# Chunk 0's gate and up products as seven block products over two halves of its tokens, in an encoder step on one NeuronCore

## Chip, core and metric

The kernel runs on one NeuronCore of a Trainium2 chip (trn2). The metric is the device time of one execution in microseconds (us). Engines are named as the profile names them: PE (TensorE, matmuls) and PEld (its weight loads), DVE (VectorE), ACT (ScalarE), POOL (GpSimd), SP (SyncE, whose queue issues nearly all DMAs here).

## What is computed

One layer of an encoder for 1152 tokens (1024 of a prompt, 128 of running streams) of width 1024:

```
x = x + 1/2 * SwiGLU_1(RMSNorm(x))
x = x + mixer(RMSNorm(x))            # gated delta rule heads and trailing-mean pooling heads
x = x + 1/2 * SwiGLU_2(RMSNorm(x))
y = RMSNorm(x)
SwiGLU(h) = (silu(h @ Wg) * (h @ Wu)) @ Wd     # Wg, Wu: 1024 x 2816, Wd: 2816 x 1024
```

The change concerns `h @ Wg` and `h @ Wu` of both SwiGLUs. All values are float32. A float32 operand is split into two parts (a rounded one and the rest, `hi` and `lo`), and a product is three matmuls: hi*hi, hi*lo, lo*hi.

## The kernel before

Tokens lie in the free dimension, in three chunks (`CHUNKS`): chunk 0 with 512 tokens, chunks 1 and 2 with 320 each. The 2816 hidden columns are 22 **rows** `f` of 128. For a row the weights are four blocks: g1, g2 (gate, first and second half of the 1024 inputs) and u1, u2 (up). A block has 4 tiles of 128x128, so that `product` (L292) of one block with one operand is 4 x 3 = 12 matmuls, each with a weight load of its own. `piece` (L275) turns a block, or the sum of two, into hi and lo: a copy on ACT (L288) and a subtraction on DVE (L289), with the sum before it on POOL (L283, L287). Pieces go round a ring of seven buffers.

**Chunks 1 and 2** are computed together by a Strassen-Winograd scheme: the two halves of the inputs by the two chunks form a 2x2 block matrix, and seven products replace eight. Its seven operands (B11, T1, B21, B22, T2, T3, T4) are sums and differences of the normalised activations. `operands` (L320) builds them, `combine` (L299) makes the sums. A row of chunks 1 and 2 thus takes 7 pieces and 7 products of 12 matmuls of 320 columns. **Chunk 0** is computed plainly: 4 products of 12 matmuls of 512 columns a row, from the operand tiles `H0` in the buffers A0 to A3.

`gate_up` (L342) runs one SwiGLU's gate and up in three stages:

- **Plain rows**, L498: rows 0 to 7 (`AHEAD = 8`), chunk 0 alone. Beside them `operands` runs in steps (`next(build)`), two steps a row.
- **Mixed rows**, L514: rows 8 to 21, each with 7 products for chunks 1 and 2 and 4 for chunk 0, one row after the other. A row has 8 pieces, since u1 alone is needed for chunk 0.
- **Rows of the other chunks**, L539: rows 0 to 7 for chunks 1 and 2, in a software pipeline: the next row's first product (`fifth`) stands before the row's sixth, and the row's last (`left_up`) after the next row's third. The `yield` at L535 stands before this stage. There the caller (`half_step`, L746) queues 14 transfers that bring chunk 0's finished rows back from DRAM into A0 to A6, for the down projection. They are issued two at a time, each pair behind a row's weight load (`pace`, L151; `load(f, 2)`).

`gated` (L357) stores the finished rows of chunks 1 and 2. Rows 0 to 7 are stored as they are. Of the others, each pair of rows goes through `combine` first, for the down projection, in steps (`step()`): 4 calls in a mixed row, 3 in a row of the last stage. A step there is a DVE operation, a copy on ACT (L370) into one of two buffers `go`, a subtraction (L371) and a DMA out. `down0` (L559) is the down projection of chunk 0. It starts with three weight loads and reads the 14 rows, and it adds its results to the `x` of chunk 0, which has stayed in the buffers x00 and x01. `down12` follows for chunks 1 and 2.

Two matters set the order of the instructions. Each engine executes its own queue in order; the framework orders the queues from the program text, so that a piece can stand ahead of an operation that comes earlier in the text but is ready later. PSUM has four tags a to d with two buffers each (`pt`).

Of the kernel before, what the change touches and what calls it, by code (L numbers as in the profile page):

```python
# [16 lines left out]
KT = D // P  # L17
# [23 lines left out]
def trunk(ctx: ExitStack, tc: tile.TileContext, xin, s0, convst, poolst, cm_in, vec_in, small_in,  # L41
# [257 lines left out]
    def combine(l1, l2, r1, r2, put):  # L299
# [7 lines left out]
        V.tensor_sub(r1, r2, r1)  # L307
# [6 lines left out]
        put("T3", r1)  # L314
        yield
        V.scalar_tensor_tensor(l2, r2, -1.0, l2, ALU.mult, ALU.subtract)
        put("T4", l2)
        yield
# [22 lines left out]

    def gate_up(wi, wg, wu, gk, H, RB, cs, ahead, norm, x0=None):  # L342
# [14 lines left out]
        def gated(f, c, t):  # L357

            q, i = f // 2, 2 * (c - 1) + f % 2
            if f < ahead:  # L360
                SY.dma_start(gk[1][q][:, i * N:(i + 1) * N], t)
                return
            rows.setdefault(q, {})[i] = t
            if len(rows[q]) < 4:
                return

            def put(name, src):
                j = DOWN.index(name)
                go = gs.get("go", 2, N)
                A.copy(go[:, 0], src)  # L370
                (V if name[0] == "B" else G).tensor_sub(go[:, 1], src, go[:, 0].bitcast(F32))  # L371
                SY.dma_start(gk[2][q - ahead // 2][j].rearrange("p (s n) -> p s n", s=2), go.bitcast(F32))

            sums.append(combine(*[rows[q][i] for i in range(4)], put))
# [10 lines left out]
        def gated0(f, pg, pu):  # L385

            sg, su, go = cs.get("sg", N0), cs.get("su", N0), cs.get("go", 2, N0)
# [5 lines left out]
            A.copy(go[:, 0], sg)  # L393
            G.tensor_sub(go[:, 1], sg, go[:, 0].bitcast(F32))  # L394
            SY.dma_start(gk[0][f].rearrange("p (s n) -> p s n", s=2), go.bitcast(F32))
            yield
# [7 lines left out]
        def fifth(w):  # L404

            be, sm, c3 = pt("c")[:, :N], gs.get("sum", 512), gs.get("c3", N)
            product(be, piece(w[2], w[3], more=(sm, w[0])), op["T1"])
            A.mul(c3, be, -1.0)
            return c3, sm

        def left_gate(al, g1, g2):

            p1, ga = gs.get("p1", N), pt("b")[:, :N]
            w1 = piece(g1)
            product(al, w1, op["B11"])
            A.copy(p1, al)
            w2 = piece(g2)
            product(ga, w2, op["B21"])
            V.tensor_add(p1, p1, ga)
            A.activation(p1, p1, AF.Silu)  # L420
            return p1, w1, w2

        def right_gate(al, sm, g2, c3):

            c2, de = gs.get("c2", N), pt("d")[:, :N]
            product(al, piece(sm), op["T2"], False)
            V.tensor_sub(c2, al, c3)
            product(de, piece(sm, g2), op["B22"])
            V.tensor_add(c2, c2, de)
            A.activation(c2, c2, AF.Silu)  # L430
            return c2

        def right_up(f, al, g1, u1, c2, c3):

            product(al, piece(g1, u1), op["T3"], False)
            V.tensor_sub(c3, c3, al)
            V.tensor_mul(c2, c2, c3)
            gated(f, 2, c2)

        def left_up(f, al, w4, p1):  # L440

            product(al, w4, op["T4"], False)
            V.scalar_tensor_tensor(p1, al, -1.0, p1, ALU.mult, ALU.mult)
            gated(f, 1, p1)
# [5 lines left out]
        op = {}  # L450
        build = operands(wi, op)
        def opening():
# [45 lines left out]
        for f in range(2 if x0 else 0, ahead):  # L498
            g1, g2, u1, u2 = load(f)
            pg, pu = pt("b")[:, :N0], pt("a")[:, :N0]  # L500
            done = gated0(f, pg, pu)
            product(pg, piece(g1), H0[0], True, False)
            product(pg, piece(g2), H0[1], False, True)
            next(done)
            product(pu, piece(u1), H0[0], True, False)
            next(build, None)
            product(pu, piece(u2), H0[1], False, True)
            next(done)
            next(build, None)
# [4 lines left out]
        for f in range(ahead, NF):  # L514
            g1, g2, u1, u2 = w = load(f)
            c3, sm = fifth(w)
            al = pt("a")[:, :N]
            p1, w1, w2 = left_gate(al, g1, g2)
            pg, pu = pt("b")[:, :N0], pt("c")[:, :N0]
            done = gated0(f, pg, pu)  # L520
            product(pg, w1, H0[0], True, False)
            product(pg, w2, H0[1], False, True)
            next(done)
            step()
            c2 = right_gate(al, sm, g2, c3)
            step()
            product(pu, piece(u1), H0[0], True, False)
            step()
            right_up(f, al, g1, u1, c2, c3)
            w4 = piece(u2)  # L530
            product(pu, w4, H0[1], False, True)
            next(done)
            step()
            left_up(f, al, w4, p1)
        yield  # L535

        last = None
        nxt = None
        for f in range(ahead):  # L539
            if not nxt:  # L540
                w = load(f, 2)
                nxt = w, fifth(w)
            (g1, g2, u1, u2), (c3, sm) = nxt
            al = pt("a")[:, :N]
            p1, _, _ = left_gate(al, g1, g2)
            if last:
                left_up(last[0], last[1], piece(last[2]), last[3])
            step()
            c2 = right_gate(al, sm, g2, c3)
            step()  # L550
            if f + 1 < ahead:
                w = load(f + 1, 2)
                nxt = w, fifth(w)
            right_up(f, al, g1, u1, c2, c3)
            last = f, al, u2, p1
            step()
        left_up(last[0], last[1], piece(last[2]), last[3])

    def down0(wd, parts, beside, done):  # L559
# [22 lines left out]
        for _ in W["raws"]:  # L582
            more(0)
# [29 lines left out]
    def down12(wd, gk, op0, beside, done):  # L613
# [15 lines left out]
        def ask(g, tags):  # L629
# [3 lines left out]
            for j, (name, tag) in enumerate(zip(DOWN, tags)):  # L633
                t = region(tag, F32R)
                op[name] = [[t[:, (2 * k + s) * N:(2 * k + s + 1) * N] for k in range(n)] for s in range(2)]
                for k in range(n):
                    pending.append(lambda t=t, j=j, k=k: SY.dma_start(
                        t[:, 2 * k * N:2 * (k + 1) * N].bitcast(F32), gk[2][q - AHEAD // 2 + k][j]))
# [75 lines left out]
    AHEAD = 8  # L714

    def half_step(wi, wg, wu, gk):
# [10 lines left out]
        cs.place(region("A4"), ("sg", N0, 2), ("su", N0, 1), ("rb", N0, 1))  # L727
# [18 lines left out]
        fetch(0, gk[0], ORDER[:14], *[f"A{i}" for i in range(7)])  # L746
        for _ in run:
            pass
        rest()

    def downs(wd, gk, src, done0=None, after0=lambda: (), done12=None, ends=lambda: None):
        op0, stage = {}, []

        def first():

            for q in range(AHEAD // 2):
# [7 lines left out]
        def sums():  # L764
            for q in range(AHEAD // 2):
# [967 lines left out]
```

## Time and profile before

| what | us |
|---|---|
| median of 3 runs (2147.2 to 2149.79) | 2149.47 |
| the profiled execution's own time | 2148.53 |
| its span in the profile | 2146.7 |
| PE busy, of the span | 2116.3 (99%) |
| DVE busy | 1528.7 (71%) |
| ACT busy | 925.8 (43%) |
| POOL busy | 498.4 (23%) |

The granted TensorE clock is at full speed in nearly all of the span. A busy PE means that matmuls are in flight; since they are pipelined, their rate is read from the start times of one block of matmuls and the next, not from the busy time or the mean duration. In the timeline, consecutive matmuls with the same output tag are merged into one row with their count, and the row's duration reaches to the end of the last, so that starts are compared with starts. The first SwiGLU's gate and up takes the stretch from about 5 to 523 us: plain rows to 99 us, mixed rows to 425 us, the other chunks' rows to 523 us. The second's takes the stretch from about 1364 to 1866 us in the same order. Down projections and the mixer fill the rest.

### The profile page before, as it was taken

The page shows a single profiled execution, that of the slowest core. Times are in us where ns is not written, and L with a number is a line of the kernel's source. Part 1 is how long each engine was busy: PE and PEld are TensorE (multiplying, and loading weights), DVE is VectorE, ACT ScalarE, POOL GpSimd, SP SyncE. Part 2 cuts the span into 40 slices and gives each one's busy share as a digit, 9 for nine tenths or more (in the row PEclk, how much of TensorE's full clock was granted, in tenths as well). Part 3 has the DMA queues.
Part 4 walks back from the last instruction along what each step waited for, and adds up shares of the span by engine and source line. Part 5 has one row for each costly group of instructions (what it writes and reads, how often), then busy time and mean ns, then how long its engine had stood idle before and what let it go on. Part 6 is the DMA issues. An engine that isn't in the chain of part 4 may idle for free.

```text
span 2146.7 us, 33093 instructions
## 1 busy us (share of the span) xinstructions
PE 2116.3 (99%) x12355; PEld 1914.3 (89%) x12355; DVE 1528.7 (71%) x2828; ACT 925.8 (43%) x1886; POOL 498.4 (23%) x471
## 2 busy tenths in 40 slices
PE   8999999999999999999999998999999999999998
PEld 7899999999889987887999998889999999988997
DVE  7966666687437887878687876786666668644877
ACT  7433333344213455645555445443333335422333
POOL 1433333351001200100111100243333344100121
PEclk9999999999999999999999999999999999999998
DMA  7333333474465732122222222433333337436572
GB/s 257 118 122 112 118 118 112 143 243 142 126 232 180 270 90 71 51 70 61 79 73 83 64 87 93 167 117 107 118 116 120 113 137 246 145 114 243 188 272 79
DMA packets 102672, 289.70 MB, mean 135 GB/s; under 512 B 16240, under 2 KB 24304, under 8 KB 102256
## 3 DMA queue, kind: packets, MB, share of 16 engines
q1 hardware_dynamic: 101216, 286.24, 39.7%
q8 instruction: 97, 1.59, 0.3%
q10 hardware_dynamic: 1296, 1.36, 0.2%
q14 instruction: 63, 0.52, 0.1%
HBM read 214.89 MB, written 72.66 MB: 134 GB/s over the span
## 4 chain that ended last, share of the span: by engine, by line
PE 89%; DVE 5%; DMA 3%; ACT 1%; POOL 1%; issue 1%; SPq 0%; POOLq 0%; DVEq 0%; ACTq 0%
PE ps_a L59 33%; PE ps_b L59 21%; PE ps_d L59 18%; PE ps_c L59 16%; DVE O L187 1%; DMA B<-g_keep 1%; PE ps_b L63 1%; DMA x<-g_keep 1%; DVE O L289 0%; DVE B L1000 0%; DVE B L769 0%; ACT O L186 0%; DVE A L1139 0%; DVE A L1140 0%; DVE x L656 0%
## 5 line engine op out<-in xcount | busy, mean ns | idle before, releaser
L59 PE MATMUL ps_a<-B,O 128*128 128x320 f32 x3040 | 504.5, 309 | 0.3
L59 PEld LDWEIGHTS ps_a<-B,O 128*128 128x128 f32 x3040 | 463.3, 188 | 9.1 <-issue 0.8
L59 PE MATMUL ps_a<-A,O 128*128 128x320 f32 (+1 forms) x1952 | 424.4, 352 | 1.7 <-DVE x L656 1.4
L59 PEld LDWEIGHTS ps_a<-A,O 128*128 128x128 f32 x1952 | 328.1, 188 | 35.3 <-ACT O L288 1.8
L289 DVE TENSOR_TENSOR O<-Q,O 128x512 fp32r<-128x512 f32 (+1 forms) x238 | 199.4, 840 | 175.6 <-ACT O L288 174.6
L59 PE MATMUL ps_b<-A,O 128*128 128x512 f32 (+1 forms) x1128 | 263.9, 387 | 5.8 <-ACT O L288 5.8
L59 PEld LDWEIGHTS ps_b<-A,O 128*128 128x128 f32 x1128 | 208.0, 188 | 46.2 <-ACT O L288 6.0
L59 PE MATMUL ps_d<-A,O 128*128 128x512 f32 x1056 | 244.2, 391 | 1.6 <-DVE x L607 0.4
L59 PEld LDWEIGHTS ps_d<-A,O 128*128 128x128 f32 x1056 | 196.8, 188 | 47.8 <-ACT O L186 3.0
L288 ACT CAST O<-Q 128x512 fp32r<-128x512 f32 (+1 forms) x238 | 143.1, 605 | 201.2 <-PE ps_c L59 54.7
L289 DVE TENSOR_TENSOR O<-R,O 128x512 fp32r<-128x512 f32 (+1 forms) x216 | 196.3, 912 | 35.7 <-ACT O L288 34.8
L59 PE MATMUL ps_d<-B,O 128*128 128x320 f32 (+1 forms) x1104 | 201.8, 329 | 1.8 <-ACT B L1027 1.0
L288 ACT CAST O<-R 128x512 fp32r<-128x512 f32 (+1 forms) x216 | 131.4, 611 | 144.9 <-PE ps_a L59 56.7
L59 PE MATMUL ps_c<-A,O 128*128 128x512 f32 (+1 forms) x816 | 187.2, 377 | 1.0 <-DVE O L289 1.0
L59 PEld LDWEIGHTS ps_d<-B,O 128*128 128x128 f32 x1104 | 171.2, 188 | 11.0 <-DVE x L1021 2.0
L59 PEld LDWEIGHTS ps_c<-A,O 128*128 128x128 f32 x816 | 145.5, 188 | 25.3 <-DVE O L289 1.8
L186 ACT CAST O<-R 128x1024 fp32r<-128x1024 f32 (+1 forms) x86 | 85.9, 1010 | 168.5 <-PE ps_d L59 127.7
L59 PE MATMUL ps_c<-B,O 128*128 128x320 f32 x912 | 144.8, 309 | 0.6 <-DVE O L289 0.6
L59 PEld LDWEIGHTS ps_c<-B,O 128*128 128x128 f32 x912 | 136.6, 188 | 1.3 <-DVE O L289 0.9
L187 DVE TENSOR_TENSOR O<-R,O 128x1024 fp32r<-128x1024 f32 (+1 forms) x86 | 101.7, 1189 | 49.2 <-ACT O L186 30.0
L59 PE MATMUL ps_b<-B,O 128*128 128x320 f32 x720 | 116.2, 309 | 0.0
L394 POOL TENSOR_TENSOR A<-A,A 128x512 fp32r<-128x512 f32 x44 | 72.8, 1654 | 161.7 <-ACT A L393 161.6
(314 smaller groups left out, 2822.8 us busy)
## 6 DMA issues: line engine op xcount, KB each, us to landing
g_keep<-x SPq DMA_DIRECT2D x98, 320.0 KB, 2.5
R<-in_wg SPq DMA_DIRECT2D x48, 512.0 KB, 3.8
R<-in_wd SPq DMA_DIRECT2D x48, 512.0 KB, 3.7
R<-in_wu SPq DMA_DIRECT2D x47, 512.0 KB, 3.7
g_keep<-A SPq DMA_DIRECT2D x44, 512.0 KB, 2.6
A<-g_keep SPq DMA_DIRECT2D x44, 512.0 KB, 5.7
B<-g_keep SPq DMA_DIRECT2D x56, 320.0 KB, 6.8
A<-g_keep SPq DMA_DIRECT2D x42, 320.0 KB, 5.1
```

Source lines behind the costliest of these rows:

```text
L59: self.put(nc.tensor.matmul(out, lhs, rhs, **k), n / 2400 + .003 if lhs.dtype == F32R else max(n, lhs.shape[-1]) / 600)
L63: self.put(nc.tensor.transpose(out, lhs, rhs), out.shape[-1] / 1200)
L186: A.copy(hi, raw)
L187: (e or V).tensor_sub(lo, raw, hi.bitcast(F32))
L288: Blocks.high = A.copy(hi, src).ins
L289: Blocks.mark = V.tensor_sub(lo, src, hi.bitcast(F32)).ins
L394: G.tensor_sub(go[:, 1], sg, go[:, 0].bitcast(F32))
```

## The change

In every SwiGLU, ten rows of chunk 0 are computed plainly instead of eight, and the other twelve by the seven-product scheme as well, with the first and second 256 tokens of chunk 0 in the place of chunks 1 and 2 (`operands0` builds its seven operands, 256 columns wide). A class `Row` replaces the row functions; it carries a tuple `pairs`: `(1,)` for chunks 1 and 2 alone, `(1, 0)` with chunk 0. A piece is split once and used for both. All rows after the plain ones stand in one pipelined loop in this order: rows 8, 9, 0, 1, 2, 3 with `(1,)`, rows 10 to 21 with `(1, 0)`, rows 4 to 7 with `(1,)`.

The seven operands of chunk 0 take the buffers A6, A0 to A3 and those of `x` itself, x00 and x01, and two of their sums pass through A4. So `x` of chunk 0 is read again from DRAM before `down0`. The transfers back (14 rows and two halves of `x`) are queued at the new `yield`, with four rows still to go, and issued three behind a row's weight load (`MOST = 3`) and two behind each of `down0`'s first weight loads.

```
+    def operands0(wi, op, RB, spare):
+        (x1, x2), n = X[0], N0 // 2
+        for k in range(KT):
+            V.scalar_tensor_tensor(xk(0, k), xk(0, k), vec[...], RB, ALU.mult, ALU.mult)
+            if k % 2:
+                yield
+        l1, l2, r1, r2 = x1[:, :, :n], x2[:, :, :n], x1[:, :, n:], x2[:, :, n:]
+        def split(name, src):
+            t = region(home[name], F32R).rearrange("p (s k n) -> p s k n", s=2, k=4)
+            A.copy(t[:, 0], src)
+            V.tensor_sub(t[:, 1], src, t[:, 0].bitcast(F32))
...
+        home = dict(zip("B11 T1 B21 B22 T2 T3 T4".split(), "A6 A0 A1 A2 A3 x00 x01".split()))
+        yield from combine(l1, l2, r1, r2, split, spare...)
...
+            def right_gate(self):
+                self.c2 = {}
+                w = piece(self.sm)
+                for c in self.pairs:
+                    self.c2[c] = gs.get("c2", N) if c else self.row[:, N0 // 2:]
+                    product(self.al[c], w, (op0, op)[c]["T2"], False)
+                    V.tensor_sub(self.c2[c], self.al[c], self.c3[c])
+                step()
+                w = piece(self.sm, self.w[1])
+                for c in self.pairs:
+                    de, c2 = self.into("b", c, w, "B22"), self.c2[c]
+                    V.tensor_add(c2, c2, de)
+                    A.activation(c2, c2, AF.Silu)
...
+        scaled = [0] * (KT // 2)
+        def built():
+            try:
+                next(build)
+            except StopIteration:
+                if scaled:
+                    next(build0)
+                    scaled.pop()
...
             product(pu, piece(u1), H0[0], True, False)
-            next(build, None)
+            built()
...
-        for f in range(ahead, NF):
...
-        for f in range(ahead):
...
+        order = [(f, (1,)) for f in (*range(RAW, ahead), *range(RAW // 2))]
+        order += [(f, (1, 0)) for f in range(ahead, NF)]
+        order += [(f, (1,)) for f in range(RAW // 2, RAW)]
+        last, row = None, Row(*order[0], 1)
+        for i, (f, pairs) in enumerate(order):
+            row.left_gate()
+            next(build0, None)
             step()
+            if last:
+                last.left_up()
+                if 0 in last.pairs and 0 not in pairs:
+                    yield
             step()
+            row.right_gate()
+            next(build0, None)
             step()
+            after = order[i + 1:i + 2]
...
+            last, row = row, Row(*after[0], MOST) if after else None
+            last.right_up()
+            next(build0, None)
             step()
+        last.left_up()
...
         for _ in W["raws"]:
-            more(0)
+            more(2)
+        rest()
...
-    AHEAD = 8
+    RAW, AHEAD = 8, 10
+    MOST = 3
...
         fetch(0, gk[0], ORDER[:14], *[f"A{i}" for i in range(7)])
+        x_new(0)
+        fetch_x(0, src)
```

`RAW` (8) takes the old `AHEAD`'s place where rows are stored as they are. The constructor of `Row` loads the weights and does the first of the seven products (T1); `left_gate`, `left_up` and `right_up` have the form of `right_gate` above, a piece and then one product for each of `pairs`.

## Rows read from the trace of the kernel before

**Rows 1.** The page's first part: busy time, share of the span, instructions of PE and DVE.

```profile
PE 2116.3 (99%) x12355; PEld 1914.3 (89%) x12355; DVE 1528.7 (71%) x2828; ACT 925.8 (43%) x1886; POOL 498.4 (23%) x471
```

**Rows 2.** PE's timeline in a mixed row of the first SwiGLU: start in us, duration in us from the first start to the last end, operation, output tag, tile shapes and count. The row of 12 matmuls on ps_c that opens the list and the one that closes it (285.26) are the first products (T1) of two rows that follow each other.

```profile
262.00 1.92 PE L59 MATMUL ps_c<-B,O 128*128 128x320 f32 x12
263.76 1.92 PE L59 MATMUL ps_a<-B,O 128*128 128x320 f32 x12
265.52 1.92 PE L59 MATMUL ps_b<-B,O 128*128 128x320 f32 x12
267.28 5.63 PE L59 MATMUL ps_b<-A,O 128*128 128x512 f32 x24
272.75 1.92 PE L59 MATMUL ps_a<-B,O 128*128 128x320 f32 x12
...
276.26 2.91 PE L59 MATMUL ps_c<-A,O 128*128 128x512 f32 x12
279.01 1.92 PE L59 MATMUL ps_a<-B,O 128*128 128x320 f32 x12
...
285.26 1.92 PE L59 MATMUL ps_c<-B,O 128*128 128x320 f32 x12
```

**Rows 3.** PE's timeline in the stage of the other chunks' rows, first SwiGLU, same columns: one row of the seven products, from its neighbour's T1 (ps_c) to the next. The block of 24 from 465.30 is T4 of one row and T2 of the next.

```profile
458.26 1.92 PE L59 MATMUL ps_c<-B,O 128*128 128x320 f32 x12
460.02 3.68 PE L59 MATMUL ps_a<-B,O 128*128 128x320 f32 x24
463.54 1.92 PE L59 MATMUL ps_b<-B,O 128*128 128x320 f32 x12
465.30 3.68 PE L59 MATMUL ps_a<-B,O 128*128 128x320 f32 x24
468.82 1.48 PE L59 MATMUL ps_d<-B,O 128*128 128x320 f32 x9
...
470.58 1.92 PE L59 MATMUL ps_c<-B,O 128*128 128x320 f32 x12
```

**Rows 4.** PE's timeline in the opening, same columns: eight matmuls with one moving column and a 128x128 weight load each, and the block after them.

```profile
23.77 0.95 PE L59 MATMUL ps_d<-ones,A 128*128 128x1 f32 x8
24.58 3.02 PE L59 MATMUL ps_a<-A,O 128*128 128x512 f32 x12
```

**Rows 5.** Busy time of the engines by stretch (start and end in us, then its length; busy us and instruction count of PE, PEld, DVE, ACT, POOL; granted clock in tenths of full, busy share of the DMA engines, GB/s). In order: the last two plain rows, the mixed rows but the first, three rows of the last stage, then that stage as a whole, the mixed rows and the last stage of the second SwiGLU.

```profile
77.43:99.19 21.76, 21.76 (x98) 18.02 (x96) 21.76 (x21) 9.72 (x14) 11.74 (x5) 1.00 0.30 96
...
122.44:424.82 302.38, 302.38 (x1718) 277.12 (x1717) 195.99 (x267) 115.74 (x227) 111.96 (x91) 1.00 0.35 120
424.82:437.14 12.32, 12.32 (x86) 12.32 (x85) 10.47 (x16) 7.45 (x16) 6.65 (x6) 1.00 0.89 318
437.14:449.46 12.32, 12.32 (x86) 12.32 (x85) 11.61 (x14) 6.20 (x12) 7.63 (x7) 1.00 0.83 271
...
461.78:474.10 12.32, 12.32 (x86) 12.32 (x85) 9.18 (x14) 5.74 (x11) 5.21 (x4) 1.00 0.58 198
...
424.82:523.40 98.58, 98.58 (x672) 98.22 (x671) 77.33 (x111) 49.08 (x94) 39.24 (x29) 1.00 0.59 194
...
1442.41:1768.05 325.64, 325.64 (x1850) 298.44 (x1849) 209.75 (x285) 123.19 (x241) 118.97 (x96) 1.00 0.34 116
1768.05:1866.60 98.55, 98.55 (x672) 98.19 (x671) 76.90 (x110) 49.11 (x94) 38.17 (x29) 1.00 0.58 194
```

**Rows 6.** Groups of instructions by line and shape over the whole program: busy us, mean ns of one, idle us of the engine before them and what ended it.

```profile
L289 DVE TENSOR_TENSOR O<-R,O 128x512 fp32r<-128x512 f32 x204 | 188.4, 927 | 35.5 <-ACT O L288 34.8 <-DMA A<-g_keep 0.2
...
L1000 DVE SCALAR_TENSOR_TENSOR B<-A,vec,B 128x512 f32<-128x512 f32 x66 | 49.3, 747 | 2.8 <-ACT B L998 2.3
...
L370 ACT CAST x<-x 128x320 fp32r<-128x320 f32 x98 | 43.7, 458 | 109.4 <-DMA g_keep<-x 70.3 <-POOL Q L283 21.9 <-DVE x L437 10.5
...
L392 DVE TENSOR_TENSOR A<-A 128x512 f32<-128x512 f32 x44 | 33.6, 763 | 2.1 <-ACT A L389 1.1
...
L388 DVE TENSOR_TENSOR A<-ps_b,A 128x512 f32<-128x512 f32 x44 | 30.3, 688 | 40.7 <-PE ps_b L59 39.7 <-ACT A L238 0.9
...
L328 DVE TENSOR_TENSOR B<-x,B 128x1280 fp32r<-128x1280 f32 x14 | 23.5, 1686 | 0.1
...
L436 DVE TENSOR_TENSOR x<-x,ps_a 128x320 f32<-128x320 f32 x44 | 21.4, 487 | 11.3 <-PE ps_a L59 11.0
...
L302 DVE TENSOR_TENSOR x<-x,x 128x320 f32<-128x320 f32 x14 | 20.6, 1471 | 0.5
...
L327 ACT CAST B<-x 128x1280 fp32r<-128x1280 f32 x14 | 17.6, 1267 | 16.5 <-DVE x L337 8.2 <-DVE x L316 6.1 <-DVE x L311 2.1
```

**Rows 7.** DVE's timeline in the last stage, first SwiGLU (start, duration, operation): the subtractions of the pieces that read `x`, which is the piece of T2, once a row.

```profile
457.41 0.69 DVE L289 TENSOR_TENSOR O<-x,O 128x512 fp32r<-128x512 f32 x1 [0.21 <-ACT O L288]
...
469.73 0.69 DVE L289 TENSOR_TENSOR O<-x,O 128x512 fp32r<-128x512 f32 x1 [0.22 <-ACT O L288]
```

**Rows 8.** Timeline of SP's queue at the end of that stage: the last row's second weight load and the down projection's first three (start in us, duration of the issue, line, what it writes and reads).

```profile
486.13 0.33 SPq L351 DMA_DIRECT2D R<-in_wu  x1
...
498.45 0.33 SPq L178 DMA_DIRECT2D R<-in_wd  x1
...
504.37 0.33 SPq L178 DMA_DIRECT2D R<-in_wd  x1
...
505.64 0.33 SPq L178 DMA_DIRECT2D R<-in_wd  x1
```

More of the change, by code (lines that the diff above doesn't have):

```diff
@@ L440, in left_up, with __init__, into, left_gate @@
[L440 to L444, printed above, removed]
+        class Row:
+            def __init__(self, f, pairs, most):
+                self.f, self.pairs = f, pairs
+                self.n = {c: (N0 // 2, N)[c] for c in pairs}
+                self.w = load(f, most)
+                self.sm = gs.get("sum", 512)
+                w = piece(self.w[2], self.w[3], more=(self.sm, self.w[0]))
+                self.c3 = {}
+                for c in pairs:
+                    be = self.into("c", c, w, "T1")
+                    self.c3[c] = (gs if c else cs).get("c3", self.n[c])
+                    A.mul(self.c3[c], be, -1.0)
+            def into(self, tag, c, w, name):
+                ps = pt(tag)[:, :self.n[c]]
+                product(ps, w, (op0, op)[c][name])
+                return ps
+            def left_gate(self):
+                self.al, self.p1, self.row = {}, {}, {}
+                w = piece(self.w[0])
+                for c in self.pairs:
+                    self.al[c] = self.into("da"[c], c, w, "B11")
+                    if c:
+                        self.p1[c] = gs.get("p1", N)
+                    else:
+                        self.row = cs.get("row", N0)
+                        self.p1[c] = self.row[:, :N0 // 2]
+                    A.copy(self.p1[c], self.al[c])
+                w = piece(self.w[1])
+                for c in self.pairs:
+                    ga, p1 = self.into("b", c, w, "B21"), self.p1[c]
+                    V.tensor_add(p1, p1, ga)
+                    A.activation(p1, p1, AF.Silu)
+            def right_gate(self):
+                self.c2 = {}
+                w = piece(self.sm)
+                for c in self.pairs:
+                    self.c2[c] = gs.get("c2", N) if c else self.row[:, N0 // 2:]
[3 more added lines that the diff above has]
+                w = piece(self.sm, self.w[1])
+                for c in self.pairs:
+                    de, c2 = self.into("b", c, w, "B22"), self.c2[c]
+                    V.tensor_add(c2, c2, de)
+                    A.activation(c2, c2, AF.Silu)
+            def right_up(self):
+                w = piece(self.w[0], self.w[2])
+                for c in self.pairs:
+                    c2, c3 = self.c2[c], self.c3[c]
+                    product(self.al[c], w, (op0, op)[c]["T3"], False)
+                    V.tensor_sub(c3, c3, self.al[c])
+                    V.tensor_mul(c2, c2, c3)
+                    if c:
+                        gated(self.f, 2, c2)
+            def left_up(self):
+                w = piece(self.w[3])
+                for c in self.pairs:
+                    p1 = self.p1[c]
+                    product(self.al[c], w, (op0, op)[c]["T4"], False)
+                    V.scalar_tensor_tensor(p1, self.al[c], -1.0, p1, ALU.mult, ALU.mult)
+                    if c:
+                        gated(self.f, 1, p1)
+                    else:
+                        store0(self.f, self.row)
@@ L557, in gate_up @@
-        left_up(last[0], last[1], piece(last[2]), last[3])
+            after = order[i + 1:i + 2]
+            if after and 0 in after[0][1] and "row" not in cs.mem:
+                for _ in build0:
+                    pass
+                cs.mem["row"] = cs.mem["sg"] + cs.mem["su"]
+                cs.mem["c3"] = [cs.mem["rb"][0][:, j:j + N0 // 2] for j in (0, N0 // 2)]
+            last, row = row, Row(*after[0], MOST) if after else None
+            last.right_up()
+            next(build0, None)
@@ L559, in down0 @@
+            step()
+        last.left_up()
+        while sums:
+            step()
     def down0(wd, parts, beside, done):
@@ L754, in first @@
         def first():
-            for q in range(AHEAD // 2):
+            for q in range(RAW // 2):
                 t = region(f"x{1 + q // 2}{q % 2}")
@@ L764, in sums @@
         def sums():
-            for q in range(AHEAD // 2):
+            for q in range(RAW // 2):
                 def put(name, src):
```

103 lines of the change are left out of this document (24 added, 79 removed).

## The prediction

> **What bounds the kernel now.** I read the page's busy times first: PE has work in 99% of the span, DVE in 71% [rows 1]. A busy PE may still run slowly, so I read its timeline by starts. In the mixed row, blocks follow each other without a gap, and one row takes 285.26 - 262.00 = 23.26 us [rows 2]. A row of the other chunks takes 470.58 - 458.26 = 12.32 us [rows 3]. The stretches by stage show PE busy for their whole length, in both SwiGLUs [rows 5]. So in the stages that the change touches nothing waits; the number of matmuls and their spacing set the time. A pipelined order of the rows can save nothing there, because there is no idle PE time to fill.
>
> The spacing: 12 matmuls of 320 columns start every 1.76 us, 146.7 ns each; 24 of 512 columns take 5.47 us, 227.9 ns each [rows 2]. The 192 further columns cost 81.2 ns, 0.423 ns a column, and each matmul has about 11 ns on top of its columns. Each has a 128x128 weight load of its own, which costs nothing visible at these lengths.
>
> **The change, part by part.**
>
> *Chunk 0 in seven products.* A mixed row had 48 matmuls of 512 columns for chunk 0; it gets 84 of 256. Columns fall from 24576 to 21504, matmuls rise by 36. No row shows 256 columns. By the slope of the two known lengths the spacing is 146.7 - 64 x 0.423 = 119.6 ns, say 120. From below it is bounded by the columns alone, 256 x 0.423 = 108 ns. The weight load is not the tighter bound: eight matmuls with one column and a full weight load each follow in 24.58 - 23.77 = 0.81 us, 101 ns apart [rows 4]. From above it is bounded by 146.7 ns, as if the shorter matmul gained nothing. I take 120, since 320 columns are the nearest row and the line through two lengths has no reason to bend while it stays above 101. The new mixed row is 84 x (146.7 + 120) = 22.40 us, 0.86 less than 23.26. With 12 such rows in each of two SwiGLUs: **-20.6 us**. By the bounds: 108 ns gives 84 x 254.7 = 21.39 us and -44.8 us; 146.7 ns gives 24.65 us and +33.3 us.
>
> *Changes of length.* Two blocks of 12 x 512 cost 2 x 2.75 = 5.50 us, one of 24 costs 5.47 [rows 2]: a change of length takes up to 0.03 us. A mixed row had three blocks of the other length and gets seven: 4 x 0.03 x 24 = 2.9 us at most, 0 at least. I take **+1.5 us**.
>
> *Rows 8 and 9* are no longer mixed. They take two plain blocks of 24 (2 x 5.47) and a row of the other chunks (12.32): 23.26 us, the same as mixed. Cost 0. Their weights are loaded twice now, 2 MB more for each SwiGLU, at 0.34 to 0.35 DMA share in the mixed stage [rows 5].
>
> *Pieces and row operations.* A mixed row has 7 pieces for 8, so DVE saves 0.93 us (L289). Three operations of 512 columns (L388 twice, L392: 2.1 us) are replaced by six of 256; scaled from 320 columns (L436, 0.49) that is 6 x 0.4 = 2.4 us [rows 6]. DVE had 195.99 of 302.38 us in the mixed stage, 65% [rows 5], and keeps that share. PE now uses one piece for 24 matmuls, every 3.2 us, where it used one per 1.76 us in places. In the pipelined order every PSUM read has at least one other pair of products between it and the matmul that needs its result (3.2 us against 0.5). Cost 0; what hides it is DVE's 35% of spare time.
>
> *Building the new operands.* This is where I expect friction. Scaling `x` is 8 operations like L1000, 0.75 us each. The combination is four sums and seven splits 1024 wide; scaled by 0.8 from L302 and L328 they are 4 x 1.18 + 7 x 1.35 = 14.2 us on DVE [rows 6]. A plain row makes two `built()` calls and the old build takes 15 steps, so in the first SwiGLU two of the four scaling steps (3.0 us) and in the second none are left for the six rows of the other chunks that follow, at three calls a row. Such a row already uses 9.18 of 12.32 us of DVE [rows 5]. First SwiGLU, three rows: 3 x 9.18 + 14.2 + 3.0 = 44.7 us of work in 36.96, short by 7.8. Second: short by 4.8. The paired sums of rows 8 and 9 add some 1.5 us within the same rows. Against that stands DVE's lead: the T2 piece is ready at 458.10 and its product is the second half of the block from 465.30, so at 467.06, 9.0 us later [rows 3, 7]. And DVE was busy for all of 21.76 us in the last two plain rows, while PE lost nothing [rows 5]. A lead of 9.0 us covers a shortage of 7.8 to 9.3 nearly whole, and three lighter rows follow. Bounds: 0 with the lead, 7.8 + 4.8 + 3.0 = 15.6 us without. I take **+2 us**. The ACT share, seven copies like L327 at 1.0 us, lies in ACT's idle half (5.74 of 12.32) and costs 0.
>
> *Faster paired sums.* `step()` is called five times a row instead of three or four. Each step needs a `go` buffer that its DMA has left; the wait for that is ACT's largest (70.3 us at L370 [rows 6]), and pieces are queued behind it. Two buffers at five steps in 12.32 us leave 4.9 us for copy, subtraction and DMA. It eats of the same lead; without the lead it would cost a microsecond or two. Cost 0, because DVE, at 10.47 and 11.61 us in the two rows with such sums before [rows 5], lost PE nothing.
>
> *Transfers back.* 16 instead of 14, and with four rows to go instead of eight. Nine go with the rows' loads, three each; seven with the down projection's first three loads, which were issued 25, 19 and 18 us before the stage's end at 523.4 [rows 5, 8]. They carry 5 x 0.5 + 2 x 1 + 3 x 0.5 = 6 MB, and 318 GB/s has been reached here [rows 5], so 19 us. SP is blocked behind a buffer only until the last mixed row's products are done. The first down unit reads eight of the 14 rows at 6 x 0.228 = 1.4 us a row, so the late six have another 10.9 us, and `x` is needed later still. Cost 0; at 200 GB/s it would be 30 us and some 5 us late in each SwiGLU, 10 in all.
>
> **The sum**: -20.6 + 1.5 + 2 = -17.1 us. The rows come from the execution of 2148.53 us (1.8 us outside its span), which lies 0.9 below the median; against the median of 2149.47 the forecast is **2132.4 us**.
>
> **The rivals.**
>
> 1. *DVE's lead is not there when the new operands are built.* If pieces are held up by their order behind the 1.2 to 1.35 us operations, PE stops for the whole shortage, 13.6 us more than I took: 2146.0 us. For it: 9.18 of 12.32 us leave little. Against it: the lead of 9.0 us and the saturated plain rows without loss. Chance 0.14.
>
> 2. *The weight load does not fit behind 256 columns* (the slower side). Its place is the 84 added matmuls of each mixed row; its price is the distance of their spacing from 120 ns; from 130.2 ns on (23.26 us / 84 - 146.7) the row is no shorter than before. At 146.7 ns the change costs 33.3 + 3.5 us: 2186.3 us. Against it: loads 101 ns apart [rows 4] and the straight line. For it: those loads had almost no moving columns beside them. Chance 0.08. The Trainium skill, "TensorE: Matmul & The Clock Gate", in the section on the mechanism of packing, lets a weight load overlap matmuls in flight only where its row group differs; 36 more loads of all 128 rows would then stand open, 36 x 0.101 - 3072 x 0.00042 = +2.3 us a row, 2205 us. The trace disagrees: by it 320 columns would be 101 + 135 = 236 ns apart, and they are 146.7; I give it 0.01 of the 0.08.
>
> 3. *The spacing is the columns alone*, 108 ns: -44.8 + 3.5, or 2108.2 us. For it: nothing but that the 11 ns on top could belong to long matmuls. Chance 0.06.
>
> 4. *The transfers back are late at the start of the down projection*: 10 us more, 2142.4 us. For it: the DMA engines were 0.83 to 0.89 busy when two fetches a row met the paired sums, and now it is three [rows 5]. Chance 0.06.
>
> **How the numbers follow.** The forecast has 0.66, with its own range from 2129 (no change-of-length cost, no stall) to 2138. With rivals 1 and 4 it makes 0.86, and the range 2125 to 2147 holds them; rivals 2 and 3 are left outside. Measurements of this kernel tell 0.2%, 4.3 us, from no change. Faster by more than that: the forecast, rivals 3 and 4, and a third of rival 1, whose price is at that border: 0.82. Within it: the rest of rival 1, 0.09. Slower: rival 2 and a little for combined stalls, 0.09.
>
> **What would show it.** Blocks of 12 matmuls of 256 columns 1.44 us apart, mixed rows 22.4 to 22.6 us apart: the main term. Gaps on PE between 125 and 165 us, ended by DVE's L289, would be rival 1; gaps in the first 20 us of the down projection ended by a DMA into A or x, rival 4; blocks 1.56 us apart or more, rival 2. The prediction is wrong if the spacing is far from 120 ns, or if PE loses over 6 us in the six rows after the plain ones.

## The result, and the profile after

The changed kernel takes **2154.64 us** (median of 16 executions, 2150.34 to 2156.90) where the kernel before took 2148.44 on the same chip (16, 2146.17 to 2150.61): a ratio of 1.0026 [1.0019, 1.0034], 0.26% slower. The prediction was 2132.4 us in a range from 2125 to 2147. The profiled execution took 2155.54 us with a span of 2153.7, 7.0 us more than the span before.

The first part of the page after, beside [rows 1]:

```profile
PE 2102.3 (98%) x13219; PEld 1942.2 (90%) x13219; DVE 1496.8 (69%) x2926; ACT 953.5 (44%) x1960; POOL 500.0 (23%) x471
```

PE has 14.0 us less work than before and the span is 7.0 us longer, so PE now waits 21 us more. Where it waits is read from its timeline. First a mixed row of the first SwiGLU, beside [rows 2]:

```profile
222.69 1.93 PE L59 MATMUL ps_c<-B,O 128*128 128x320 f32 x12
224.45 1.60 PE L59 MATMUL ps_c<-A,O 128*128 128x256 f32 x12
225.89 1.93 PE L59 MATMUL ps_a<-B,O 128*128 128x320 f32 x12
227.65 1.60 PE L59 MATMUL ps_d<-x,O 128*128 128x256 f32 x12
...
245.09 1.19 PE L59 MATMUL ps_c<-B,O 128*128 128x320 f32 x7
...
469.09 1.93 PE L59 MATMUL ps_c<-B,O 128*128 128x320 f32 x12
```

A block of 12 with 256 columns takes 225.89 - 224.45 = 1.44 us, 120.0 ns each, and a row 245.09 - 222.69 = 22.40 us. The twelve rows leave nothing over: from their first T1 (203.17) to the first T1 behind them (469.09) are 265.92 us, which is 84 x 1.76 + 82 x 1.44 with not a tenth left. The intended saving, 24 x 0.86 = 20.6 us, is there in full.

Next the same view of the six rows of the other chunks that run ahead of the mixed ones, where the new operands are built: first SwiGLU, then the two ends of that stretch in the second. The bracket is PE's idle time before the block and what ended it.

```profile
126.14 1.92 PE L59 MATMUL ps_c<-B,O 128*128 128x320 f32 x12
...
145.72 2.02 PE L59 MATMUL ps_a<-B,O 128*128 128x320 f32 x12 [1.52 <-ACT x L459]
...
152.55 3.78 PE L59 MATMUL ps_a<-B,O 128*128 128x320 f32 x24 [1.29 <-DVE x L473]
...
158.49 4.00 PE L59 MATMUL ps_a<-B,O 128*128 128x320 f32 x24 [0.40 <-DVE x L487]
...
167.46 3.78 PE L59 MATMUL ps_a<-B,O 128*128 128x320 f32 x24 [1.45 <-DVE x L473]
...
203.17 1.92 PE L59 MATMUL ps_c<-B,O 128*128 128x320 f32 x12
...
1470.05 1.92 PE L59 MATMUL ps_c<-B,O 128*128 128x320 f32 x12
...
1512.83 5.32 PE L59 MATMUL ps_a<-B,O 128*128 128x320 f32 x24 [2.07 <-DVE x L473]
...
1549.67 1.92 PE L59 MATMUL ps_c<-B,O 128*128 128x320 f32 x12
```

The 3.42 us behind the gap at 1512.83, with the columns of [rows 5]:

```profile
1513.39:1516.81 3.42, 3.42 (x15) 3.42 (x14) 3.31 (x6) 1.30 (x3) 2.67 (x2) 0.50 0.73 230
```

From the first T1 to that of the first mixed row there are 40 blocks of 12 (two of the 42 are carried past it), 40 x 1.76 = 70.4 us. The stretches take 77.03 and 79.62 us: **6.6 and 9.2 us lost**. Of the 9.2, 1.7 are not waiting: behind the longest gap (2.07 us) the granted clock is 0.50 from 1513.39 to 1516.81, and the block of 24 takes 1517.99 - 1512.83 = 5.16 us, where 24 at full clock take 3.52. No gap of 0.4 us or more is ended by a piece (L289). They are ended by operations that read ps_a, onto which the next product is then added: the copy L459 behind B11, the subtraction L473 behind T2 and L487 behind T3. What these had ahead of them, in the timeline of all engines:

```profile
139.11 3.37 POOL L287 TENSOR_TENSOR x<-Q,R 128x512 f32<-128x512 f32 x1 [6.48 <-issue]
...
142.43 2.26 POOL L283 TENSOR_TENSOR Q<-R,R 128x512 f32<-128x512 f32 x1
...
144.72 0.62 ACT L288 CAST O<-Q 128x512 fp32r<-128x512 f32 x1 [3.51 <-POOL Q L283]
145.25 0.42 ACT L459 COPY x<-ps_a 128x320 f32<-128x320 f32 x1
...
150.49 0.48 DVE L498 SCALAR_TENSOR_TENSOR x<-ps_a,x 128x320 f32<-128x320 f32 x1
150.89 1.21 DVE L355 TENSOR_TENSOR x<-A,x 128x1024 fp32r<-128x1024 f32 x1
152.02 0.48 DVE L473 TENSOR_TENSOR x<-ps_a,x 128x320 f32<-128x320 f32 x1
```

At 152.02 L473 starts right behind one of the new splits (L355); PE resumes at 152.55. At 145.25 the copy L459 stands on ACT behind a piece's cast (L288), which waited 3.51 us for two sums on POOL. What is left of the building for the six rows stands in the first three (in the first SwiGLU it ends at 152.1 us). DVE is nearly full there, while over all six rows it is busy for 70.8 of 77.0 and 67.6 of 79.6 us. The first three rows of either SwiGLU, with the columns of [rows 5]:

```profile
126.14:164.09 37.95, 34.70 (x229) 33.43 (x228) 36.44 (x46) 19.32 (x36) 20.16 (x12) 1.00 0.31 100
1470.05:1508.84 38.79, 34.70 (x229) 33.44 (x228) 35.16 (x45) 19.23 (x36) 19.20 (x12) 1.00 0.29 101
```

Two more losses lie outside these rows. In the opening, the first lines after, then the same place before:

```profile
43.12 1.40 DVE L347 SCALAR_TENSOR_TENSOR x<-x,vec,A 128x512 f32<-128x512 f32 x2
44.45 0.15 DVE L232 TENSOR_SCALAR rt<-ps_d 128x3 f32<-128x3 f32 x1
44.67 2.70 POOL L233 TENSOR_TENSOR rt<-rt,vec 128x3 f32<-128x3 f32 x1 [4.49 <-DVE rt L232]
47.43 0.93 PE L59 MATMUL ps_d<-ident,rt 128*128 128x128 f32 x6 [3.10 <-POOL rt L233]
```

```profile
40.97 0.15 DVE L232 TENSOR_SCALAR rt<-ps_d 128x3 f32<-128x3 f32 x1
41.20 0.86 POOL L233 TENSOR_TENSOR rt<-rt,vec 128x3 f32<-128x3 f32 x1 [2.50 <-DVE rt L232]
42.67 0.83 PE L59 MATMUL ps_d<-ident,rt 128*128 128x128 f32 x6
```

The new scaling operations (L347) are ready early, so the framework puts them into the opening, ahead of a chain of three short steps on which PE waits. And at the start of the down projection, after and before:

```profile
523.75 2.02 PE L59 MATMUL ps_a<-B,O 128*128 128x320 f32 x12 [0.58 <-DVE x L487]
...
526.95 11.87 PE L59 MATMUL ps_d<-A,O 128*128 128x512 f32 x51 [1.18 <-ACT O L186]
...
540.23 6.16 PE L59 MATMUL ps_d<-A,O 128*128 128x512 f32 x24 [1.40 <-ACT O L186]
```

```profile
521.62 0.86 PE L59 MATMUL ps_d<-A,O 128*128 128x512 f32 x3
522.37 2.02 PE L59 MATMUL ps_a<-B,O 128*128 128x320 f32 x12
```

Before, the down projection's first matmuls ran ahead of the last product and filled the wait for it; after, the split that its first matmuls read (L186) comes only when the last product is done. The reason is in the ring of seven piece buffers. A SwiGLU makes 8 + 32 + 22 x 7 = 194 pieces, where it made 8 + 24 + 14 x 8 + 8 x 7 = 200. The last one, number 193, falls into O4 (193 mod 7), one of the two buffers (O4, O5) that the first split overwrites; before it was O3.

**The ledger**, in us: mixed rows -20.6; six rows +6.6 and +9.2 (with 1.7 of the lower clock); opening chain +3.7 (first SwiGLU only); start of the down projection +3.7 and +2.9; the start of the program +1.5 (a block that starts at 31.09 before and 32.59 after; kernels whose program starts alike had 31.58 to 34.61, so this place varies by itself; of the kernel before there is one trace). The sum is +7.0, the span's difference; shifts of up to 0.5 us that are not listed cancel.

### The profile page after: what moved, and what is told of

The parts are those of the page before. It is cut to its first block, busy times and chain, and to the rows that moved or that the text cites. A ratio compares the mean times of both kernels' runs of the same rounds, so it can differ in the third digit from the quotient of the medians.

```text
span 2153.7 us, 34922 instructions
## 1 busy us (share of the span) xinstructions
PE 2102.3 (98%) x13219; PEld 1942.2 (90%) x13219; DVE 1496.8 (69%) x2926; ACT 953.5 (44%) x1960; POOL 500.0 (23%) x471
## 5 line engine op out<-in xcount | busy, mean ns | idle before, releaser
L59 PE MATMUL ps_d<-A,O 128*128 128x512 f32 (+1 forms) x1632 | 320.9, 353 | 6.0 <-ACT O L186 4.8
L59 PEld LDWEIGHTS ps_d<-A,O 128*128 128x128 f32 x1632 | 270.5, 189 | 52.9 <-ACT O L186 8.0
L289 DVE TENSOR_TENSOR O<-Q,O 128x512 fp32r<-128x512 f32 (+1 forms) x238 | 185.9, 785 | 119.6 <-ACT O L288 118.6
L288 ACT CAST O<-Q 128x512 fp32r<-128x512 f32 (+1 forms) x238 | 143.1, 605 | 175.4 <-PE ps_b L59 44.8
L59 PE MATMUL ps_b<-A,O 128*128 128x256 f32 (+2 forms) x1128 | 207.1, 334 | 5.7 <-ACT O L288 5.7
L289 DVE TENSOR_TENSOR O<-R,O 128x512 fp32r<-128x512 f32 (+1 forms) x204 | 155.6, 768 | 66.6 <-ACT O L288 66.1
L59 PE MATMUL ps_b<-B,O 128*128 128x320 f32 x1248 | 200.9, 309 | 0.0
L59 PEld LDWEIGHTS ps_b<-A,O 128*128 128x128 f32 x1128 | 175.4, 191 | 25.9 <-ACT O L288 5.9
L59 PEld LDWEIGHTS ps_b<-B,O 128*128 128x128 f32 x1248 | 186.4, 188 | 0.0
L288 ACT CAST O<-R 128x512 fp32r<-128x512 f32 (+1 forms) x204 | 123.9, 612 | 120.8 <-PE ps_d L59 35.5
L186 ACT CAST O<-R 128x1024 fp32r<-128x1024 f32 (+1 forms) x86 | 85.8, 1008 | 176.5 <-PE ps_d L59 128.0
L59 PE MATMUL ps_d<-B,O 128*128 128x320 f32 (+1 forms) x576 | 117.4, 347 | 1.8 <-ACT B L1087 1.0
L59 PEld LDWEIGHTS ps_d<-B,O 128*128 128x128 f32 x576 | 92.1, 189 | 11.0 <-DVE x L1081 2.0
L389 ACT CAST x<-x 128x320 fp32r<-128x320 f32 x98 | 44.8, 458 | 98.5 <-DMA g_keep<-x 33.2
```

What stands on the lines that cost most here:

```text
L59: self.put(nc.tensor.matmul(out, lhs, rhs, **k), n / 2400 + .003 if lhs.dtype == F32R else max(n, lhs.shape[-1]) / 600)
L186: A.copy(hi, raw)
L288: Blocks.high = A.copy(hi, src).ins
L289: Blocks.mark = V.tensor_sub(lo, src, hi.bitcast(F32)).ins
```

## The experiments

The theory after the result: the new operands cost DVE more than these six rows have, and what PE waits for is behind them in a queue. Its rival: the rows have the time, but the operations come in bunches of three, and it is the bunch that holds up an operation reading PSUM. Beside them stand the ring, the opening, and the transfers back of the prediction's rival 4. Each kernel starts from the changed one; ratios are to the kernel before on the same chip (medians 2148.26 to 2148.82), with 95% intervals. "Loss" is that in the six rows, first and second SwiGLU, read from the one profiled execution of each kernel; where the granted clock fell to 0.50 within them, the text says so.

**1. Without building.** The kernel leaves out the scaling, the sums and the splits; chunk 0's products read the first 256 columns of the other chunks' operands.

```
- build0 = operands0(wi, op0, RB, cs.base[:, :4 * (N0 // 2)])
+ build0 = iter(())
...
+ op0[name] = [[t[:, :N0 // 2] for t in half] for half in op[name]]
```

> This kernel leaves out the building of chunk 0's seven operands (no scaling of x, no sums, no splits); the seven products read the first 256 columns of the other chunks' operands instead, so matmuls, pieces and row operations stay. Theory: the building costs PE 6.7 + 9.2 us in the six rows after the plain ones and 3.7 us in the opening. Expected with it: the six rows lose under 1.5 us in each SwiGLU, the opening's 3 us gap on ps_d<-ident is gone, about 2154.6 - 18 = 2136 us. Rival (the denser paired sums, or the ring and PSUM order of the new rows, stop PE): the six rows still lose 5 us or more each, 2146 us or more.

2136.75 us, 0.9943 [0.9931, 0.9956]; loss 0.0 and 0.0, and the opening has no gap. The building is the cause of the loss in the six rows and of the opening's gap. The time stays 8.5 us above the 2128.2 that the saving alone would leave (2148.8 - 20.6), and the down projection's start keeps its gaps, so that they have another cause. Five windows of 12 us from 121.00 on (PE, PEld, DVE, ACT, POOL busy, as in [rows 5]), of which two and the sum are shown, tell what a row asks for without it:

```profile
145.00:157.00 12.00, 12.00 (x84) 12.00 (x83) 11.12 (x17) 5.87 (x13) 5.04 (x4) 1.00 0.45 138
157.00:169.00 12.00, 12.00 (x84) 12.00 (x83) 9.84 (x14) 6.04 (x13) 7.75 (x6) 1.00 0.53 185
...
sum 60.00, PE 60.00 PEld 59.88 DVE 50.03 ACT 30.52 POOL 31.94; mean PE 12.00 PEld 11.98 DVE 10.01 ACT 6.10 POOL 6.39
```

10.01 of 12.00 us is 10.3 in a row of 12.32, not the 9.18 of [rows 5] that the prediction used.

**2. The ring of pieces started at its seventh buffer.** `n` counts the pieces, and a piece takes buffer `n` mod 7; the ring keeps its seven buffers. Started at 6, the last piece falls into O3 as before ((6 + 193) mod 7).

```
  bl = Blocks([...])
+ bl.n = 6
```

> The ring of piece buffers starts at its seventh buffer instead of its first, so that after 194 pieces the last piece stands in O3, as after 200 before, and not in O4, which the down projection's first split takes. Theory (the first split waits for the last product because it shares a buffer with the last piece): the 1.2 to 1.4 us gaps ahead of the down projection go, and with them the late loads behind that split; down projection's first 50 us lose about 1.5 us instead of 4.9 and 4.2, about 2148.5 us. Rival (the 16 transfers back and the second reading of x are what is late): no change, 2154 to 2155 us.

2149.69 us, 1.0000 [0.9991, 1.0009]; loss 6.2 and 7.4. The start of the down projection looks as before again, and one gap stays:

```profile
522.27 0.86 PE L59 MATMUL ps_d<-A,O 128*128 128x512 f32 x3
523.02 2.02 PE L59 MATMUL ps_a<-B,O 128*128 128x320 f32 x12
524.88 11.07 PE L59 MATMUL ps_d<-A,O 128*128 128x512 f32 x48
538.81 7.48 PE L59 MATMUL ps_d<-A,O 128*128 128x512 f32 x24 [2.86 <-ACT O L186]
```

The ring's phase is shown as the cause of the first split's wait. In the gap at 538.81 the split on ACT is queued behind the copy of a staged row (L829) that waits for its DMA: a remnant of rival 4, read from the trace and not tried by itself. The granted clock is 0.50 from 540.31 to 543.73, so that the block behind this gap takes 7.48 us.

**3. The scaling held to its place.**

```
+ with tc.issue_after(Blocks.mark):
      V.scalar_tensor_tensor(xk(0, k), xk(0, k), vec[...], RB, ALU.mult, ALU.mult)
```

> The eight scaling operations of chunk 0's x are held behind the latest piece on DVE, so that they cannot run in the opening. Theory (hoisted scaling delays the short chain DVE, POOL, PE of the other chunk's norm): the 3 us gap at 44 us goes, the six rows lose as much as before or a little more in the first SwiGLU, 2151 to 2152 us. Rival (the gap comes from the loads of x in the opening, by chance): the gap stays, 2154 to 2155 us.

2152.51 us, 1.0021 [1.0012, 1.0030]. The opening's chain goes on at 43.16 without a wait (47.43 in the changed kernel), and the 3.7 us there are gone. The loss is 9.4 and 7.4, 2.8 more in the first SwiGLU. The scaling does not fall into the six rows: it now runs in the last plain rows, from 102.28 us to just behind the first T1 at 121.44, and the first split (L356 here) stands behind it.

```profile
119.22 2.44 DVE L348 SCALAR_TENSOR_TENSOR x<-x,vec,A 128x512 f32<-128x512 f32 x2
```

Of the 2.8 us, 1.7 are the clock, which is 0.50 from 128.92 to 132.34, right behind a gap at 128.79. So most of the 3.7 us is lost again a little later.

**4. The building in single steps**, two a row in place of three, on top of 3: each sum and each split a step of its own. The scaling takes two steps instead of four, which brings it to 105.0 to 112.6 us, so the edit bears on the bunching and on what DVE still has to do when the six rows begin.

```
- yield from combine(l1, l2, r1, r2, split, ...)
+ for do in ops:    # 11 single sums and splits
+     with tc.issue_after(Blocks.mark):
+         do()
+     yield
...
- next(build0, None)    # behind right_up()
```

> The building is cut into single DVE operations, two a row over all six rows (instead of one or two operations a step, three steps a row), each held behind the latest piece; scaling in two steps, held likewise. Same work. Theory (row operations that read PSUM stand in DVE's and ACT's queues behind pairs of 1.2 us operations; it is their bunching, not the total, that stops PE): the six rows lose 1 to 5 us instead of 6.7 and 9.2, the opening's gap is gone, about 2141 us. Rival (DVE lacks the throughput in these rows: 14.2 us more in six rows of 12.32 with 9.2 used, which would fit, or contention with POOL makes it not fit): still 6 us or more each, 2150 us or more.

2146.82 us, 0.9989 [0.9980, 0.9998]; loss 5.9 and 5.7. That is 3.4 and 1.7 less than in 3, and 1.7 of the 3.4 are the clock, which stays full here. The loss is far from none, and it lies above the expected 1 to 5, as the total lies between the expected 2141 and the rival's 2150: the bunches were a part, not all. DVE is full while PE waits; the first line has all six rows of the first SwiGLU:

```profile
124.15:200.50 76.35, 71.90 (x482) 70.40 (x480) 72.47 (x90) 38.73 (x75) 39.75 (x27) 1.00 0.40 128
...
147.00:159.00 12.00, 10.99 (x74) 10.49 (x73) 11.88 (x14) 4.96 (x11) 7.73 (x5) 1.00 0.49 163
159.00:172.00 13.00, 10.66 (x71) 10.16 (x71) 12.93 (x17) 7.60 (x15) 8.20 (x6) 1.00 0.52 167
```

**5. The ring's start and single steps.** Both edits, 2 and 4.

> The ring start of e2 and the spread, held building of e4 together. If the two losses are separate places, their gains add: e2 gained 5.0 us, e4 7.8 us against the changed kernel, so about 2142 us. Rival (the time given back at the down projection's start is lost again behind the late staged rows, or DVE in the six rows is what counts whatever the order): 2145 us or more.

2141.41 us, 0.9970 [0.9958, 0.9982]; loss 6.0 and 5.7. The two add up.

**6. The low halves on ACT.** Kernel 4, with the splits' subtraction replaced by a second copy, so that the low parts are not computed.

```
- V.tensor_sub(t[:, 1], src, t[:, 0].bitcast(F32))
+ A.copy(t[:, 1], src)
```

> As e4, but the low parts of chunk 0's seven operands are copies on ACT instead of subtractions on DVE (so the low parts are not computed; matmuls unchanged). It takes about 7 x 1.3 = 9 us off DVE in the six rows and puts 7 on ACT. Theory now (e4 left DVE busy for 11.6 to 11.9 of each 12 us: the six rows ask for more DVE time than they have, 6 x 10.3 + 14 + 3 = 79 against 74 us): with 70 us asked the six rows lose under 2 us in each SwiGLU instead of 6.0 and 5.8, about 2139 us. Rival (the wait is the latency of single 1.2 us operations ahead of a PSUM read, or ACT's queue): 4 us or more lost in each, 2143 us or more.

2137.96 us, 0.9952 [0.9940, 0.9965]; loss 0.4 and 2.2, the second a little over the expected 2. The places, the steps and their number are those of 4; DVE has less work and ACT more:

```profile
123.50:194.34 70.84, 70.64 (x481) 70.39 (x480) 60.92 (x84) 44.16 (x81) 37.16 (x28) 1.00 0.43 137
...
147.00:159.00 12.00, 12.00 (x84) 12.00 (x84) 10.92 (x17) 7.15 (x14) 6.79 (x5) 1.00 0.48 153
159.00:171.00 12.00, 12.00 (x84) 11.99 (x83) 10.37 (x14) 8.50 (x17) 7.36 (x6) 1.00 0.55 190
```

Of the two it is DVE's time that counts in kernel 4: there DVE works for 72.5 us in rows for which PE needs 70.4, and here for 60.9. POOL's sums are not what differs: the longest L287 of this kind takes 1.76 us in 4 and 1.75 here. How much of DVE's time in 4 is operations that POOL lengthens (last section) is not told apart.

**7. The rows with paired sums last**, on top of 5: the first six rows are 0 to 5, which have none.

```
- order = [(f, (1,)) for f in (*range(RAW, ahead), *range(RAW // 2))]
+ order = [(f, (1,)) for f in range(RAW - 2)]
...
- order += [(f, (1,)) for f in range(RAW // 2, RAW)]
+ order += [(f, (1,)) for f in (*range(RAW, ahead), RAW - 2, RAW - 1)]
```

> As e5, and the rows of the other chunks in another order: rows 0 to 5 ahead of the mixed rows, rows 8, 9, 6, 7 behind them. Rows 0 to 5 are stored as they are, so that no paired sums (about 3.4 us of DVE, with ACT, POOL and DMA) fall into the six rows in which the operands are built. Theory (DVE time in the six rows): asked for falls to 6 x 9.2 + 14 + 3 = 72 of 74 us, the six rows lose 1 to 4 us instead of 6, about 2137 us, below both kernels. Rival: the sums do not matter, 2142 us as e5; or the paired sums of rows 8 and 9 now meet the transfers back in the last four rows and PE stops there instead.

2146.97 us, 0.9986 [0.9977, 0.9995], a miss by 10 us. Loss 2.6 and 1.9 as expected; the end pays for it, as the second half of the expected rival has it:

```profile
504.45 3.79 PE L59 MATMUL ps_a<-B,O 128*128 128x320 f32 x24 [1.56 <-DVE x L484]
...
537.62 8.34 PE L59 MATMUL ps_d<-A,O 128*128 128x512 f32 x23 [4.09 <-ACT O L186]
```

The paired sums of rows 8 and 9 now run beside the transfers back. The split L186 stands on ACT behind copies of a staged row, the first of which waits for its DMA until 529.00 (522.29 in 5); that the paired sums are what delays this DMA is likely, not shown. The granted clock is 0.50 for 6.8 us around the gap at 537.62 and for 3.4 us at the same place of the second SwiGLU, which makes some 4.5 of the 10 us (half of PE's busy time in them).

**8. The same order alone**, on the changed kernel.

> The changed kernel with the row order of e7 alone (building bunched as it was, ring as it was). Theory (time on DVE): the six rows lose 3 to 5 us instead of 6.7 and 9.2, about 2148 us. Rival (bunching of long operations ahead of PSUM reads in the first three rows, whatever else DVE does): 6 us or more lost in each as before, since rows 8 and 9 added their sums only from the third row on, 2152 us or more.

2158.97 us, 1.0046 [1.0034, 1.0059]; loss 3.3 and 4.5 as the theory says, the total a miss by 11 us. The start of the down projection has longer gaps than the changed kernel, as in 7, and three stretches of 3.4 us at half the clock, one of them behind the gap in the opening.

**9. Paired sums late among the six**, on top of 5.

```
- order = [(f, (1,)) for f in (*range(RAW, ahead), *range(RAW // 2))]
+ order = [(f, (1,)) for f in (*range(RAW // 2), *range(RAW, ahead))]
```

> As e5, with the six rows in the order 0, 1, 2, 3, 8, 9 instead of 8, 9, 0, 1, 2, 3; rows 4 to 7 stay behind the mixed rows. The paired sums of rows 8 and 9 then fall into the first mixed rows, where DVE is busy for some 65% only, and the last four rows stay as in e5. Theory (DVE time in the six rows, and nothing new at the end): the six rows lose 2 to 3 us each as in e7, instead of 6.0 and 5.7, the down projection's start as in e5, about 2134.5 us, the fastest of all. Rival (the sums stop PE wherever they fall): the first mixed rows lose some us, 2139 us or more.

**2133.90 us, 0.9931 [0.9917, 0.9944]**: 0.7% less than the kernel before, with the whole computation in it. Loss 2.9 and 2.1, in the slowest of its five executions (2139.11). Rows 0 to 3 come first and have no paired sums; rows 8 and 9 with theirs follow, and what is left of the sums falls into the first mixed rows, where PE loses nothing (second fence, 22 us):

```profile
124.46 1.92 PE L59 MATMUL ps_c<-B,O 128*128 128x320 f32 x12
...
166.84 3.75 PE L59 MATMUL ps_a<-B,O 128*128 128x320 f32 x24 [1.62 <-ACT x L470]
...
197.72 1.92 PE L59 MATMUL ps_c<-B,O 128*128 128x320 f32 x12
```

```profile
200.00:222.00 22.00, 22.00 (x165) 22.00 (x164) 13.86 (x22) 9.63 (x23) 9.85 (x9) 1.00 0.39 132
```

**10. That order alone**, on the changed kernel.

> The changed kernel with the six rows in the order 0, 1, 2, 3, 8, 9 alone. Theory: the six rows lose 3 to 5 us as in e8 instead of 6.7 and 9.2, the opening and the end as in the changed kernel, 2146 to 2149 us. Rival (the loss in e8's six rows was lower by chance): 2152 us or more.

2150.18 us, 1.0001 [0.9992, 1.0010]; loss 3.5 and 4.5, in one of its fastest executions (2145.19). The total is 1.2 us above the expected range and below the rival's 2152. Without the ring's other start and the held scaling the order brings the program back to the time before and no further.

## Why the prediction was wrong

- **Chunk 0 in seven products**: right. 120 ns taken, 120.0 measured, row 22.40 us as worked out. Rivals 2 and 3 fall with it: a weight load of 128 rows fits behind 256 columns, and the 11 ns on top of the columns stay. The Trainium skill's rule of the row groups ("TensorE: Matmul & The Clock Gate", the mechanism of packing), by which 2205 us would have come, does not describe these loads if taken alone; the same section lets the engine also pull ahead a load into a background weight buffer, which would fit, and no run here shows that buffer. The 2205 us leave out the 3.5 us that the prediction adds in its other rivals; with them it is some 2208.
- **Changes of length**: 1.5 us taken, 0 measured.
- **Pieces and row operations, rows 8 and 9**: right for the mixed rows, which lose nothing.
- **Building the new operands: the step that failed.** 2 us taken, 15.8 measured, of which 1.7 are the lower clock and 14.1 waiting. What failed is "A lead of 9.0 us covers a shortage of 7.8 to 9.3 nearly whole". The lead is that of the pieces, which are made from weights and can be early. An operation that reads a product from PSUM has no lead; it cannot start before its product ends, and a product that follows soon waits for it. It stands in the same queue behind the building. All gaps of 0.4 us and more in the six rows are of that kind. The comparison with the plain rows, where DVE was full and PE lost nothing, did not bear on this: plain rows have no product that is added onto a PSUM tile which another engine has to read first. The shortage itself was about right in the first SwiGLU and too low in the second. The 9.18 us a row came from a row without paired sums; with them it is 10.3 (experiment 1), 3.4 us more in three rows, where the prediction added 1.5. The 3.0 us of scaling, on the other hand, are not in these rows: in the changed kernel the first SwiGLU's scaling runs from 41 to 68 us, and in no kernel does it start behind the first T1. That makes 3 x 10.3 + 14.2 - 37.0 = 8.1 us, where the prediction had up to 9.3 and up to 6.3. (For the same reason the 79 us that the text before experiment 6 puts against 74 is 3.0 too high.) That the loss of 15.8, with 1.7 of the clock in it, comes out so near the bound of 15.6 is in part luck. Experiment 1 shows that the building is what PE waits for, 10 that the paired sums add to it, and 6 that in kernel 4 it is the building's time on DVE; how much of that time is DVE and POOL lengthening each other stays open.
- **Faster paired sums**, "Cost 0": wrong at the same place. Moving them behind the building, with nothing else changed, takes 3.1 and 4.8 us off the loss (experiment 10; 1.7 of the 4.8 are the clock). Not only their time on DVE goes with them: ahead of the longest gap, at 1512.83, a copy of these sums (L389) waits 1.32 us on ACT for a DMA to leave its `go` buffer, and pieces stand behind it. That is the friction that the prediction named and put at 0.
- **Transfers back**, "Cost 0": the stage border did cost 3.7 and 2.9 us, though mostly for a reason the prediction had not listed, the buffer into which the last piece falls (experiment 2). A late staged row shows once the ring starts elsewhere.
- **Not foreseen**: the scaling in the opening, 3.7 us. The text counted scaling steps only by the calls that ask for them, and did not ask where the framework puts an operation that is ready sooner. The clock, too, has no term: a wait in these rows cost up to 1.7 us more than it lasted.
- **Rival 1** came at its price, with another mechanism than it names (L473, L459 and L487, not L289); it and the two unlisted terms, 10.3 us together, and the 1.5 of the start turn a saving of 20.6 us into a loss of 7.0.

## What to carry to other kernels

When work is moved into a stage that is full of matmuls, add up each engine's demand over that stage from its own rows, and separate operations that can run ahead (made from weights) from those that read a product: only the first have a lead to spend. Where a ring of buffers passes from one stage to the next, work out in which buffer the last entry falls whenever the count of entries changes. And look for short chains, such as a norm's, that an operation without a place of its own can get in front of. Where PE has waited, read the granted clock of the next few us before the whole loss is put down to the wait.

## What the runs showed of the hardware

- Behind some waits TensorE's granted clock is 0.50 for a few us, the lower of its two levels (1.2 GHz). In the changed kernel this follows the wait of 2.07 us that ends at 1512.83: 24 matmuls of 320 columns take 5.16 us instead of 3.52. The other waits of these rows, 0.39 to 1.52 us, are not followed by it.
- Matmuls of 256 columns, each with a 128x128 weight load, start every 120.0 ns, in alternation with 320 columns at 146.7, and the alternation costs nothing in 265.92 us.
- POOL and DVE operations are longer beside each other. POOL's sum L287 has a median of 1.29 us and took 3.37 beside the building; without the building (experiment 1) the longest of the same kind is 1.30; DVE's split L355 has 1.21 at its shortest and 1.92 to 2.32 at its longest. That fed the wait of 3.51 us on ACT. The Trainium skill ("SBUF — State Buffer", on the two separate sides) has POOL and a DVE operation with two SBUF inputs exclude each other at a shared pair of ports; the rows agree that both lengthen, and no run here tells how the pair is passed on.
- In the opening, POOL's operation on 128x3 (L233) took 2.70 us after, where DVE's operations followed each other without a gap, and 0.86 before, where DVE was idle for 0.5 us of it.
